# Moving the last rope-query transposes, the context's own attention and some due times in a one-core hybrid attention step

## The chip, the core and the metric

The kernel runs on one core of one Trainium2 chip. The metric is the device time of one execution in microseconds, here always called the time; the profile adds a span, which runs from the first to the last instruction of the program on that core. Five engines work side by side, each through a queue of its own in fixed order: TensorE (PE, with its weight loads as PEld), VectorE (DVE), ScalarE (ACT), GpSimd (POOL) and SyncE (SP), which here issues DMAs only.

## What is computed

One step of a diffusion trunk for 1024 latent tokens and 128 context tokens, all fp32, width 1024, one layer. Both token sets pass the same weights:

```python
h = _rmsnorm(x, norm_g) * (1 + scale) + shift           # scale, shift from the conditioning vector
u, v, g_a, c_q, c_kv, k_rope, g_b = _split_in(h @ w_in)
a_out = _chunk_mlp(u, v, w_s, b_s, g_v) * silu(g_a)      # gated mixing of positions, chunks of 128
q = (_rmsnorm(c_q, q_norm_g) @ w_uq)                     # 4 heads, 128 nope and 64 rope columns each
ckv = _rmsnorm(c_kv, kv_norm_g)                          # latent keys and values, 128 wide
attn = softmax over (1024 latent keys with rotated k_rope, 256 cached context keys unrotated)
y = concat([a_out, attn * silu(g_b)]) @ w_o
x = x + gate * y                                         # then a last rmsnorm
```

The context tokens attend only to themselves (one tile of 128 queries by 128 keys, four heads). The query of a head is kept as three pieces that are multiplied with the keys: the nope part folded with the key expansion, the rotated rope part and the raw rope part.

## The kernel before

Nine tiles of 128 tokens: tiles 0 to 7 are latent, tile 8 (`NS`) is the context. Every fp32 matrix product is done as three fp32r products (high by high, high by low, low by high), so each operand has a high half, made by an ACT or POOL cast, and a low half, made by a DVE subtraction (`lo_of`, L109). Nothing is scheduled by the machine here: instructions stand on each engine in the order in which the Python calls them, and the code steers that order with a clock of its own. `run((cost, fn))` (L204) calls a step and moves the clock by `cost`; `later(dt, fn)` (L164) puts a follow-up, such as an eviction, at a due time; `need(key)` (L194) pulls waiting follow-ups forward until a key is made; `merged(a, b)` (L209) interleaves two lists of steps by their costs.

The stages, by the time in the profile: from 0 to 246 us normalisation, modulation and the projections of group A and the gates; from 246 to 310 us the loop over tiles (L1044 to L1058) that projects `z` (c_q, c_kv, k_rope), with z's transposes, the folding of weights, rope queries and nope queries of earlier tiles beside it; from 310 to 322 us a hand-written list (L1074 to L1092) that closes this phase; from 322 to 508 us the attention; then the output projection.

The names that matter below. `zacc8` is the PSUM bank with z of tile 8. `cq_transpose(t)` (L927) transposes c_q of a tile into bank `cqT`; ACT writes the high half `cqh`, DVE the low half `cql`. `q_rope(t)` (L957) multiplies them with the rope weights into bank `qr`; ACT copies it out (`qun`), DVE and POOL rotate it (`qr1`). `q_rope_T(t)` (L983) transposes the result into bank `qrT` and splits it in two parts: ACT cast L1001, DVE subtraction L1002, for the even heads and for the odd ones. `keys(t0, n, kind)` (L1007) transposes latent keys (kind 0, `kch`, `kcl`) or rope keys (kind 1, `krh`, `krl`) of n tiles through bank `kT`. `q_nope` gives `qn`. Until 322 us PSUM is divided in a ring of six banks (`psa`) and a ring of two (`pst`); a new tile in a ring waits until the bank's last reader is done.

In the attention a head of a latent tile has three score steps: `lat(0)` and `lat(1)`, five matmuls of 512 columns each into `s1`, and `con`, five of 256 into `s2` (L1141 to L1145). DVE then takes the two maxima (L1116, L1119) and the shift (L1120), ACT the exponentials (L1126, two per head, each followed by a read-out of the row sum), DVE the reciprocal and POOL scales the row (L1132). `value_stream` transposes two heads' rows in five groups (`pT`, L1188, in the ring `pst` of two banks), splits them (ACT `ph`, L1192; DVE `pl`, L109) and multiplies them with the values into bank `o`.

The context's own attention is `own_steps()` with four steps: `score` (20 matmuls of 128 columns into `s8`), `tr` (four transposes of the scaled rows `e8` into `pT8`), `av` (three matmuls into `o8`) and `up` (the value expansion into `at8`, also from the ring `pst`). They are placed between the score steps of the first heads by hand:

```python
own = own_steps()
first = [s_ for i in range(LEAD) for s_ in score_steps(*heads[i])]
merged(first[:4] + own[:1] + first[4:], [])
...
    if c == 0:
        sc = sc[:3] + own[1:2] + sc[3:5] + own[2:3] + sc[5:] + own[3:]
```

With `LEAD = 2`, `first` holds heads 0 and 1 of tile 0; the loop's round `c` adds two more heads and, from round 1 on, the value stream of the pair of heads before.

Of the kernel before, what the change touches and what calls it, by code (L numbers as in the profile page):

```python
# [18 lines left out]
P = 128  # L19
NT = 9  # L20
NS = 8
# [70 lines left out]
def tile_hymba_step(ctx: ExitStack, tc: tile.TileContext, I, O):  # L92
# [777 lines left out]
    def z_stats(t, ps):  # L870
# [52 lines left out]
        later(0.35, squares)  # L923
        later(0.9, rope_key)
        later(1.5, scales)

    def cq_transpose(t):  # L927
        last = t == NT - 1
        ps = (psa if last else pst).tile([P, 512], F32, tag="acc" if last else "t", name=f"cqT{t}")
        for q in range(2):  # L930
            T.transpose(ps[:, q * P : (q + 1) * P], zt[t][:, q * P : (q + 1) * P], ident)
        src = ps[:, 0:256].rearrange("p (q c) -> p q c", q=2)
        dh = cqh[:, :, t * P : (t + 1) * P]

        def low():
            lo_of(cql[:, :, t * P : (t + 1) * P], src, dh)
            made.add(("cq", t))

        later(0.4, lambda: S.copy(dh, src))
        later(0.85, low)  # L940
# [14 lines left out]
    rot = {}  # L955

    def q_rope(t):  # L957
# [4 lines left out]
        un = zp.tile([P, 4, 64], F32, tag="qun", name=f"qun{t}", bufs=3)  # L962
        rot[t] = [un]

        def raw():
            S.copy(un, ps[:, :256].rearrange("p (h r) -> p h r", h=4))
# [3 lines left out]
            r1 = zp.tile([P, 4, 64], F32, tag="qr1", name=f"qr1{t}", bufs=2)  # L970
# [10 lines left out]
        later(0.85, raw)  # L981

    def q_rope_T(t):  # L983
# [3 lines left out]
        late = t == NS  # L987
# [19 lines left out]
    def keys(t0, n, kind):  # L1007
        need(*[("k", t0 + i) for i in range(n)])
        ps = (psa if t0 == 4 else pst).tile([P, 512], F32, tag="acc" if t0 == 4 else "t", name=f"kT{t0}{kind}")
        for i in range(n):  # L1010
            src = kvn[:, t0 + i, :] if kind == 0 else krd[:, t0 + i, :, :].rearrange("p a r -> p (a r)")
            T.transpose(ps[:, i * P : (i + 1) * P], src, ident)
        sl = slice(t0 * P, (t0 + n) * P)
        dh, dl = (kch, kcl) if kind == 0 else (krh, krl)
        later(0.11 * n + 0.1, lambda: S.copy(dh[:, sl], ps[:, : n * P]))
        later(0.25 * n + 0.3, lambda: lo_of(dl[:, sl], ps[:, : n * P], dh[:, sl]))
# [23 lines left out]
    with tc.manual_schedule(engines=engines):  # L1040
# [3 lines left out]
        for t in range(NT):  # L1044
# [21 lines left out]
        vl = kv.tile([P, 11, P], F32R, tag="vl", name="vl")  # L1066
        for i, (dh, dl) in enumerate(((kch, kcl), (krh, krl))):
# [3 lines left out]
        later(11.0, lambda: pool_copy(cv[0], ctxr[:, 2, :]))  # L1071
        later(11.0, lambda: G.tensor_tensor(cv[1], ctxr[:, 2, :], f32(cv[0]), op=ALU.subtract))
        for t0, c in ((8, 1), (0, 4), (4, 4)):
            later(11.5, lambda t0=t0, c=c: values(t0, c))  # L1074
        for cost, fn in (
# [8 lines left out]
            (1.05, lambda: q_nope(2, 0)),  # L1084
            (0.15, lambda: keys(8, 1, 1)),
            (0.15, lambda: keys(8, 1, 0)),
            (1.05, lambda: q_nope(2, 1)),
            (1.05, lambda: q_nope(2, 2)),
            (0.25, lambda: q_rope_T(8)),
# [322 lines left out]
    with tc.manual_schedule(engines=engines):  # L1412
# [28 lines left out]
        merged(first[:4] + own[:1] + first[4:], [])  # L1441
        for c in range(len(pairs)):
            sc = [s_ for i in (2 * c + LEAD, 2 * c + LEAD + 1) if i < len(heads) for s_ in score_steps(*heads[i])]
            if c == 0:
                sc = sc[:3] + own[1:2] + sc[3:5] + own[2:3] + sc[5:] + own[3:]
# [3 lines left out]
            if 2 * c + LEAD + 1 == 11:  # L1449
                c_wo, wo = opened("wo", side="left")  # L1450
# [211 lines left out]
```

## Time and profile before

| | us |
|---|---|
| time, median of 3 runs | 629.55 (629.07 to 630.03) |
| time of the profiled execution | 629.15 |
| its span | 627.2 |
| PE busy | 612.7 (98%) |
| DVE busy | 359.7 (57%) |
| ACT busy | 265.2 (42%) |
| POOL busy | 177.8 (28%) |

The page gives busy time by engine, the chain that ended last and the costliest groups; the trace behind it answers for a stretch of time, for one engine's instructions in order with the idle time before each, and for single tiles. The profiled execution's time is 0.40 us below the median of the runs, and 1.95 us above its own span, which is the work around the program. In a timeline row the first number is the start in us from the span's beginning, the second how long the row took; a row `x2` holds two instructions. Matmuls overlap: the next one starts before the row of the last has ended, so the pace of PE is read from start to start.

### The profile page before, as it was taken

To read this page: it belongs to the slowest core of one execution; us is meant where nothing else is said; L and a number is where in the kernel's file an instruction comes from. 1 tells how busy PE (TensorE), PEld (TensorE's weight loads), DVE (VectorE), ACT (ScalarE), POOL (GpSimd) and SP (SyncE) were. 2 spreads that over 40 slices of the span, in tenths; PEclk is the share of its full clock that TensorE was granted. 3 is DMA by queue.
4 is the path that set the end of the run, shared out by engine and by line. 5 is a ranking of instruction groups with operands and counts; after the bars stand their busy time and mean duration, and the time that the engine had idled before them with its cause. 6 is when DMAs were issued, how large, how long until landed. Compare 5 with 4: busy or idle time off the path is not lost.

```text
span 627.2 us, 9800 instructions
## 1 busy us (share of the span) xinstructions
PE 612.7 (98%) x3703; PEld 552.5 (88%) x3703; DVE 359.7 (57%) x839; ACT 265.2 (42%) x638; POOL 177.8 (28%) x217
## 2 busy tenths in 40 slices
PE   8999999999999999999989999999999999999995
PEld 7568889999999999999977999999999988888884
DVE  4773456049556100456677666776666754487655
ACT  8655753112111111565666555546656543132212
POOL 2551123344535500433444212332222341000001
PEclk9999999999999999999999999999999999999999
DMA  8992010042321203000010000001101123423311
GB/s 324 401 355 68 1 33 2 2 169 82 116 103 62 93 4 114 27 2 1 1 41 1 2 0 1 2 2 34 34 1 33 36 68 103 167 100 135 112 56 67
DMA packets 15966, 46.32 MB, mean 74 GB/s; under 512 B 1952, under 2 KB 4912, under 8 KB 15920
## 3 DMA queue, kind: packets, MB, share of 16 engines
q1 hardware_dynamic: 15776, 45.51, 20.6%
q8 instruction: 29, 0.48, 0.3%
q10 hardware_dynamic: 144, 0.20, 0.1%
q14 instruction: 17, 0.14, 0.1%
HBM read 40.87 MB, written 4.83 MB: 73 GB/s over the span
## 4 chain that ended last, share of the span: by engine, by line
PE 92%; DVE 3%; ACT 2%; DMA 1%; issue 1%; SPq 0%; ACTq 0%
PE tp L716 6%; PE tp L156 6%; PE tp L155 6%; PE tp L157 6%; PE pT L1188 5%; PE w L1435 5%; PE w L1436 5%; PE w L1437 5%; PE o L1212 3%; PE o L1214 3%; PE s L1141 3%; PE o L1213 3%; PE s L1143 3%; PE s L1144 3%; PE s L1142 3%; PE s L1145 3%
## 5 line engine op out<-in xcount | busy, mean ns | idle before, releaser
L109 DVE TENSOR_TENSOR pl<-pT,ph 128x512 fp32r<-128x512 f32 x81 | 55.5, 687 | 48.2 <-ACT ph L1192 48.0
L1132 POOL TENSOR_SCALAR e<-e,rs 128x1280 f32<-128x1280 f32 x32 | 42.8, 1338 | 137.5 <-DVE rs L1131 118.8
L157 PE MATMUL tp<-area,w2l 128*128 128x384 f32 x216 | 72.5, 336 | 0.0
L155 PE MATMUL tp<-area,w2h 128*128 128x384 f32 x216 | 72.5, 336 | 0.0
L156 PE MATMUL tp<-area,w2h 128*128 128x384 f32 x216 | 72.5, 336 | 0.0
L1126 ACT ACTIVATE e<-s,nb,scl 128x256 f32<-128x256 f32 x64 | 56.1, 880 | 36.5 <-DVE nb L1120 36.4
L1192 ACT CAST ph<-pT 128x512 fp32r<-128x512 f32 x80 | 45.3, 588 | 43.5 <-PE pT L1188 40.6
L1188 PE MATMUL pT<-ident,e 128*128 128x128 f32 x320 | 47.9, 272 | 0.6 <-DVE pl L109 0.6
L1212 PE MATMUL o<-ph,vh 128*128 128x256 f32 x160 | 47.8, 299 | 0.0
L109 DVE TENSOR_TENSOR w2l<-w2r,w2h 128x1024 fp32r<-128x1024 f32 x12 | 19.8, 1656 | 45.5 <-POOL w2h L112 45.5
L1214 PE MATMUL o<-ph,vl 128*128 128x256 f32 x160 | 44.9, 281 | 0.0
L1213 PE MATMUL o<-pl,vh 128*128 128x256 f32 x160 | 44.7, 280 | 0.0
L1437 PE MATMUL w<-area,ml 128*128 128x512 f32 (+1 forms) x114 | 43.2, 379 | 0.0
L1188 PEld LDWEIGHTS pT<-ident,e 128*128 128x128 f32 x320 | 37.5, 140 | 4.3 <-DVE pl L109 1.5
L155 PEld LDWEIGHTS tp<-area,w2h 128*128 128x128 f32 x216 | 40.5, 188 | 0.6 <-issue 0.5
L156 PEld LDWEIGHTS tp<-area,w2h 128*128 128x128 f32 x216 | 40.5, 188 | 0.2
L157 PEld LDWEIGHTS tp<-area,w2l 128*128 128x128 f32 x216 | 40.5, 188 | 0.0
L1116 DVE TENSOR_REDUCE m<-s 128x1 f32<-128x1024 f32 x32 | 38.9, 1216 | 2.3 <-PE s L1145 2.3
L1141 PE MATMUL s<-kch,area 128*128 128x512 f32 (+2 forms) x100 | 39.0, 390 | 0.1
L716 PE MATMUL tp<-area,w2h 128*128 128x384 f32 x144 | 37.4, 340 | 0.0
L1144 PE MATMUL s<-krh,area 128*128 128x512 f32 (+2 forms) x100 | 35.4, 354 | 0.0
L1143 PE MATMUL s<-kch,area 128*128 128x512 f32 (+2 forms) x100 | 35.4, 354 | 0.0
(308 smaller groups left out, 1576.0 us busy)
## 6 DMA issues: line engine op xcount, KB each, us to landing
ada<-in_ada_ss SPq DMA_DIRECT2D x16, 512.0 KB, 10.1
w2r<-in_w_t SPq DMA_DIRECT2D x12, 512.0 KB, 3.6
x<-in_x SPq DMA_DIRECT2D x9, 512.0 KB, 5.8
xr<-in_x SPq DMA_DIRECT2D x9, 512.0 KB, 4.6
adag<-in_ada_g SPq DMA_DIRECT2D x8, 512.0 KB
wor<-in_w_o SPq DMA_DIRECT2D x8, 512.0 KB, 3.4
out_y<-y SPq DMA_DIRECT2D x8, 512.0 KB, 2.7
wvr<-in_w_v SPq DMA_DIRECT2D x8, 256.0 KB, 8.9
```

Of the source, the lines that this page charges most:

```text
L109: V.tensor_tensor(lo, src, f32(hi), op=ALU.subtract)
L155: T.matmul(ps, wh, xh, start=j == 0, stop=False)
L156: T.matmul(ps, wh, xl, start=False, stop=False)
L157: T.matmul(ps, wl, xh, start=False, stop=j == n - 1)
L716: T.matmul(tps[i, g][:, :GW], w_[i][:, k, :], x_[k, g], start=k == 0 and j == 0, stop=k == NK - 1 and j == 2)
L1126: S.activation(e[:, sl], src, AF.Exp, bias=nb, scale=scl[:, t : t + 1], accum_out=su[:, i : i + 1])
L1141: T.matmul(ps, qh_, kch[:, sl], start=True, stop=False)
L1188: T.transpose(ps[:, w : w + P], es[t, h][:, c * P : (c + 1) * P], ident)
L1212: T.matmul(o, vh[:, kt, :], ph[:, sl], start=c == 0, stop=False)
L1213: T.matmul(o, vh[:, kt, :], pl[:, sl], start=False, stop=False)
L1214: T.matmul(o, vl[:, kt, :], ph[:, sl], start=False, stop=c == n - 1)
L1437: T.matmul(ps, b, woh[k][:, c0:c1], start=False, stop=k == NK - 1)
```

## The change

Five things are done; no arithmetic is added or taken away, and the number of instructions on PE, DVE and POOL stays the same.

1. In the loop over the z tiles, the c_q transposes, the weight fold and the rope-query transposes of a round become one step (`full`) in place of three that were spread among z's chunks.
2. The rope queries' transposes of tile 6 go from the closing list into the last round of that loop, those of tile 8 between the score steps of heads 0 and 1, and those of tile 7 into round 1 of the attention. The copies that they read, for tiles 7 and 8, get a pool of their own (`ra`), which is closed before the pool of the output weights is opened in its place; so the first load of output weights now also waits for POOL's last use of it.
3. `keys(0, 4, ·)` takes its banks from the ring of six in place of the ring of two.
4. Due times: for tile 8 the squares of z and what follows them come later; the c_q split of tile 8 is due sooner; the rope copies of tiles 7 and 8 are due later, the first low half of the keys too; the values' copies on POOL are due sooner.
5. The own attention: `score` goes from behind `lat(0)` of head 1 to behind all of head 1; `tr` stays behind head 2; `av` goes behind all of head 3; `up` goes behind `lat(0)` of head 4, into the round that also runs the first value stream.

```diff
         later(0.3, lambda: S.copy(zs, ps[:, :448]))
-        later(0.35, squares)
+        later(1.2 if t == NS else 0.35, squares)
         later(0.9, rope_key)
-        later(1.5, scales)
+        later(2.2 if t == NS else 1.5, scales)
...
-        later(0.4, lambda: S.copy(dh, src))
-        later(0.85, low)
+        later(0.05 if last else 0.4, lambda: S.copy(dh, src))
+        later(0.42 if last else 0.85, low)
...
-        later(0.85, raw)
+        later({7: 2.6, 8: 1.2}.get(t, 0.85), raw)
...
-        late = t == NS
+        late = t >= 7
         tp = (pst if late else psa).tile([P, 512], F32, tag="t" if late else "acc", name=f"qrT{t}")
...
-        ps = (psa if t0 == 4 else pst).tile([P, 512], F32, tag="acc" if t0 == 4 else "t", name=f"kT{t0}{kind}")
+        ps = (psa if t0 < 8 else pst).tile([P, 512], F32, tag="acc" if t0 < 8 else "t", name=f"kT{t0}{kind}")
...
+            full = []
             if t >= 1:
-                beside.append((0.25, lambda t=t: cq_transpose(t - 1)))
+                full.append((0.25, lambda t=t: cq_transpose(t - 1)))
             if 1 <= t < 5:
-                beside.append((0.45, lambda t=t: fold(t - 1)))
+                full.append((0.45, lambda t=t: fold(t - 1)))
             if t >= 3:
-                beside.append((0.45, lambda t=t: q_rope_T(t - 3)))
+                full.append((0.45, lambda t=t: q_rope_T(t - 3)))
+            if full:
+                beside.append((sum(f[0] for f in full), lambda full=full: [f[1]() for f in full]))
...
             if t == NT - 1:
+                beside.append((0.45, lambda: q_rope_T(t - 2)))
                 beside.append((0.75, lambda: q_rope(t - 1)))
...
-            (0.45, lambda: q_rope_T(6)),
-            (0.45, lambda: q_rope_T(7)),
             (0.75, lambda: q_rope(8)),
...
-            (0.25, lambda: q_rope_T(8)),
...
-        merged(first[:4] + own[:1] + first[4:], [])
+        merged(first[:3] + [(0.25, lambda: q_rope_T(8))] + first[3:] + own[:1], [])
...
             if c == 0:
-                sc = sc[:3] + own[1:2] + sc[3:5] + own[2:3] + sc[5:] + own[3:]
+                sc = sc[:3] + own[1:2] + sc[3:] + own[2:3]
+            if c == 1:
+                sc = sc[:1] + own[3:] + sc[1:4] + [(0.45, lambda: q_rope_T(7))] + sc[4:]
...
             if 2 * c + LEAD + 1 == 11:
+                closed(c_ra)
                 c_wo, wo = opened("wo", side="left")
```

Three places show what this does to the order of instructions. A digit behind a name is the tile, or the tile and the head (`e01` is head 1 of tile 0).

First TensorE, right behind the last matmul of z, in the kernel before: the keys' transposes, the c_q transposes of tile 8, the rope queries' transposes, then the rope query of tile 8.

```order
L1012 MATMUL kT00_3165<-ident_75,kvn_2366 128x128 x4
L1012 MATMUL kT01_3176<-ident_75,krd_2367 128x128 x4
L931 MATMUL cqT8_3190<-ident_75,z8_3142 128x128 x2
L1012 MATMUL kT40_3194<-ident_75,kvn_2366 128x128 x4
L1012 MATMUL kT41_3203<-ident_75,krd_2367 128x128 x4
L992 MATMUL qrT6_3218<-ident_75,qr16_3073 128x128 x2
L992 MATMUL qrT6_3218<-ident_75,qun6_3058 128x128 x2
L992 MATMUL qrT7_3225<-ident_75,qr17_3155 128x128 x2
L992 MATMUL qrT7_3225<-ident_75,qun7_3138 128x128 x2
L155 MATMUL qr8_3232<-wrh_2358,cqh_2354 128x256
```

The same place in the changed kernel:

```order
L1015 MATMUL kT00_3166<-ident_75,kvn_2366 128x128 x4
L1015 MATMUL kT01_3177<-ident_75,krd_2367 128x128 x4
L931 MATMUL cqT8_3187<-ident_75,z8_3149 128x128 x2
L1015 MATMUL kT40_3192<-ident_75,kvn_2366 128x128 x4
L1015 MATMUL kT41_3214<-ident_75,krd_2367 128x128 x4
L155 MATMUL qr8_3222<-wrh_2358,cqh_2354 128x256
```

Eight transposes have left: four went ahead of z's end, four into the attention.

Second ScalarE at the start of the attention, before: `e8` stands between the exponentials of heads 0 and 1, and the copy of `o8` between those of heads 2 and 3.

```order
L1126 ACTIVATE e00_3338,su00_3336<-s2_3320,nb00_3335,scl_92 128x256
L1126 ACTIVATE e00_3338,su00_3336<-s100_3323,nb00_3335,scl_92 128x1024
L1332 ACTIVATE e8_3386,su8_3389<-s8_3355,nb8_3388,scl_92 128x128 x4
L1126 ACTIVATE e01_3385,su01_3383<-s2_3320,nb01_3382,scl_92 128x256
L1126 ACTIVATE e01_3385,su01_3383<-s101_3345,nb01_3382,scl_92 128x1024
L1349 CAST ph8_3442<-pT8_3437 128x512
L1126 ACTIVATE e02_3427,su02_3425<-s2_3320,nb02_3424,scl_92 128x256
L1126 ACTIVATE e02_3427,su02_3425<-s102_3405,nb02_3424,scl_92 128x1024
L1366 COPY e8_3386<-o8_3466 128x512
L1126 ACTIVATE e03_3465,su03_3463<-s2_3320,nb03_3462,scl_92 128x256
L1126 ACTIVATE e03_3465,su03_3463<-s103_3446,nb03_3462,scl_92 128x1024
```

And in the changed kernel, up to the same pair of heads:

```order
L1133 ACTIVATE e00_3325,su00_3323<-s100_3310,nb00_3322,scl_92 128x1024
L1004 CAST area2_119<-qrT8_3332 64x2x128
L1133 ACTIVATE e01_3357,su01_3355<-s2_3307,nb01_3354,scl_92 128x256
L1133 ACTIVATE e01_3357,su01_3355<-s101_3337,nb01_3354,scl_92 128x1024
L1339 ACTIVATE e8_3399,su8_3402<-s8_3368,nb8_3401,scl_92 128x128 x4
L1356 CAST ph8_3436<-pT8_3431 128x512
L1133 ACTIVATE e02_3418,su02_3416<-s2_3307,nb02_3415,scl_92 128x256
L1133 ACTIVATE e02_3418,su02_3416<-s102_3393,nb02_3415,scl_92 128x1024
L1133 ACTIVATE e03_3459,su03_3457<-s2_3307,nb03_3456,scl_92 128x256
L1133 ACTIVATE e03_3459,su03_3457<-s103_3440,nb03_3456,scl_92 128x1024
L1373 COPY e8_3399<-o8_3469 128x512
L1199 CAST ph00_0_3489<-pT00_0_3484 128x512
```

The four exponentials of `e8` now stand behind both of head 1, the copy of `o8` behind both of head 3, and the second part of the rope queries of tile 8 (L1004; the first part stands two rows ahead of the piece) between heads 0 and 1. On DVE the maxima of head 1 likewise stand ahead of those of `s8`.

Third TensorE around the last step of the own attention, before: `at8` follows the `con` step of head 3, ahead of head 4.

```order
L1362 MATMUL o8_3466<-ph8_3442,vl_3153 128x512
L1141 MATMUL s2_3320<-kch_3148,area0_117 128x256
L1142 MATMUL s2_3320<-kcl_3149,area0_117 128x256
L1143 MATMUL s2_3320<-kch_3148,area0_117 128x256
L1144 MATMUL s2_3320<-krh_3150,area0_117 128x256
L1145 MATMUL s2_3320<-krl_3151,area0_117 128x256
L1375 MATMUL at8_3480<-e8_3386,wuv_2364 128x128 x4
L1141 MATMUL s110_3489<-kch_3148,area0_117 128x512
```

And now:

```order
L1195 MATMUL pT00_1_3491<-ident_75,e00_3325 128x128
L1195 MATMUL pT00_1_3491<-ident_75,e01_3357 128x128
L1382 MATMUL at8_3499<-e8_3399,wuv_2364 128x128 x4
L1195 MATMUL pT00_2_3510<-ident_75,e00_3325 128x128
L1195 MATMUL pT00_2_3510<-ident_75,e01_3357 128x128
```

`at8` now stands behind the first half of head 4's scores and behind the first two groups of transposes of the value stream (`pT00_0`, four transposes, stands just ahead of this piece, and `pT00_1` begins with two more like the first two rows); `pT00_0`, `pT00_1` and `at8` follow each other in the ring of two banks. `s110` is the first half of head 4.

More of the change, by code (lines that the diff above doesn't have):

```diff
@@ L1070, in tile_hymba_step @@
         cv = [v_[:, 9:, :].rearrange("p a r -> p (a r)") for v_ in (vh, vl)]
[L1071 to L1072 removed]
+        later(9.0, lambda: pool_copy(cv[0], ctxr[:, 2, :]))
+        later(9.0, lambda: G.tensor_tensor(cv[1], ctxr[:, 2, :], f32(cv[0]), op=ALU.subtract))
         for t0, c in ((8, 1), (0, 4), (4, 4)):
[L1074 removed]
+            later(9.5, lambda t0=t0, c=c: values(t0, c))
         for cost, fn in (
```

15 lines of the change are left out of this document (10 added, 5 removed).

## The prediction

> **What bounds the kernel now.** I read the page first, then the busy time by stretches, then TensorE's timeline where it was not full. In the second fence the columns are the stretch, its length, and the busy time (with instruction counts) of PE, PEld, DVE, ACT and POOL, then the granted clock.
>
> ```profile
> PE 612.7 (98%) x3703; PEld 552.5 (88%) x3703; DVE 359.7 (57%) x839; ACT 265.2 (42%) x638; POOL 177.8 (28%) x217
> ```
>
> ```profile
> 246.00:310.00 64.00, 63.99 (x368) 59.85 (x367) 35.64 (x117) 34.40 (x103) 21.92 (x61) 1.00 0.04 10
> 310.00:346.00 36.00, 32.76 (x200) 27.90 (x200) 26.02 (x58) 23.14 (x58) 16.12 (x22) 1.00 0.06 19
> 346.00:480.00 134.00, 134.00 (x935) 123.56 (x934) 90.75 (x190) 76.61 (x159) 36.01 (x33) 1.00 0.03 11
> ```
>
> TensorE sets the end: it is full while z is projected and full in the attention, and short by 3.24 us between 310 and 346, where the change works. Work that merely changes its place on a full TensorE costs nothing, and a microsecond in which TensorE waits is a microsecond at the end. So the sum is one of waits. Those of TensorE in that stretch stand in brackets:
>
> ```profile
> 313.89 0.39 PE L155 MATMUL qr<-wrh,cqh 128*128 128x256 f32 x1 [0.18 <-ACT cqh L939]
> 315.36 0.39 PE L157 MATMUL qr<-wrh,cql 128*128 128x256 f32 x1 [0.96 <-DVE cql L109]
> 320.81 0.44 PE L992 MATMUL qrT<-ident,qun 128*128 128x128 f32 x2 [1.16 <-DVE krl L109]
> 322.40 0.50 PE L1141 MATMUL s<-kch,area 128*128 128x512 f32 x1
> 338.47 1.16 PE L1375 MATMUL at<-e,wuv 128*128 128x128 f32 x8 [0.42 <-ACT e L1366]
> 343.23 0.66 PE L1188 MATMUL pT<-ident,e 128*128 128x128 f32 x4 [0.41 <-DVE pl L109]
> ```
>
> That is 0.18 + 0.96 + 1.16 + 0.42 + 0.41 = 3.13 us: it is the most that this stretch can give, 0.5% of the time. The first matmul after a wait also takes about 0.1 us longer than its like, which I count with each wait.
>
> **The front, 310 to 322 us.** With the rope queries' transposes gone, TensorE still stops at the third matmul of the rope query of tile 8, which needs `cql` from DVE.
>
> ```profile
> 312.60 0.49 ACT L888 ACTIVATE zw<-ssz,epsb 128x1 f32<-128x1 f32 x2
> 312.99 0.58 ACT L1015 CAST krh<-kT 128x512 fp32r<-128x512 f32 x1
> 313.45 0.39 ACT L939 CAST cqh<-cqT 128x256 fp32r<-128x256 f32 x1
> 310.33 0.37 ACT L966 COPY qun<-qr 128x256 f32<-128x256 f32 x1 [1.50 <-PE qr L157]
> ```
>
> ```profile
> 310.80 0.42 DVE L975 TENSOR_TENSOR qr<-qr,rope 128x256 f32<-128x256 f32 x1 [0.93 <-ACT qun L966]
> 314.89 0.41 DVE L109 TENSOR_TENSOR cql<-cqT,cqh 128x256 fp32r<-128x256 f32 x1
> ```
>
> Before, the cast `cqh` starts at 313.45, behind two roots (312.60 to 312.99) and `krh` (to 313.45). Now those 0.85 us stand behind it, while four transposes of tile 6 (about 0.11 us each, row of eight at 340.63 below) delay z's end by 0.43: `cqh` starts at 313.03. But on DVE the rotation of tile 7 now stands ahead of `cql`, and it waits for the copy `qun`, which stands behind `cqh` (0.39) and `krh` (0.46): 313.88, plus 0.47 from copy to rotation as above, plus 0.42, plus 0.41 for `cql`: 315.18, and TensorE at 315.24 instead of 315.36. The new wait for the bank of z of tile 8, at `kT41`, for which the late squares answer, ends before that and adds nothing.
>
> From there to the first score before: 322.40 − 315.36 = 7.04. Of it go the wait of 1.16, 0.22 for the transposes of tile 8, about 0.1 of idle time ahead of the first score and about 0.1 of restart. The first score starts at 315.24 + 5.46 = 320.70, 1.7 us earlier. Of that 0.65 (six transposes) is only put off, and the first score's own restart of 0.1 goes too. Net **−1.15**. Ends: −1.6 if rows overlap as closely as `zw` and `krh` do, −0.7 if DVE loses another half.
>
> **The rope query of tile 8, now inside the attention.** Its two parts are split by ACT and DVE; the first and last rows give the shorter form (64x256) as their least duration, the longer (64x512) as their median, in ns.
>
> ```profile
> L1001 ACT CAST area<-qrT x18: 366/582/597, 269.4 to 321.7; 64x512 fp32r<-64x512 f32 x16, 64x256 fp32r<-64x256 f32 x2
> L1002 DVE TENSOR_TENSOR area<-qrT,area x18: 419/685/694, 272.1 to 322.8; 64x512 fp32r<-64x512 f32 x16, 64x256 fp32r<-64x256 f32 x2
> ```
>
> ```profile
> 328.59 0.19 ACT L1126 ACTIVATION_READ_ACCUMULATOR e<-s,nb,scl 128x1 f32 x1
> ```
>
> ```profile
> 325.43 0.40 PE L1141 MATMUL s<-kch,area 128*128 128x512 f32 x1
> 326.57 0.22 PE L1141 MATMUL s<-kch,area 128*128 128x128 f32 x1
> ```
>
> I keep the clock of before, with the first score at 322.40. Head 0's exponentials end with the read-out at 328.59; the next ACT row can start at about 328.69, and that is now the second part: 0.37, then DVE 0.42 and 0.42: 329.53 and 329.95 with 0.05 of handing over. TensorE now has, ahead of `s8`, the other half of head 1 (326.57 − 325.43 = 1.14), its `con` (0.62, from 2.90 for a head as below less two halves) and 0.22 of transposes: `s8` starts at 328.55 and its first rope matmul, the fourth, at 328.88. It waits until 329.59: **+0.7**, and 0.1 of restart. The cover that hid these splits before was the nope queries; who waits behind the matmul is all of the attention. Ends 0.5 and 0.95.
>
> **The chain from `s8` to `e8`.** The rows that it is made of:
>
> ```profile
> 329.81 0.15 DVE L1130 TENSOR_TENSOR rs<-su 128x1 f32<-128x1 f32 x1
> ...
> 330.17 1.23 DVE L1116 TENSOR_REDUCE m<-s 128x1 f32<-128x1024 f32 x1
> ```
>
> ```profile
> 330.07 0.46 ACT L1332 ACTIVATE e<-s,nb,scl 128x128 f32<-128x128 f32 x1 [1.29 <-issue]
> ...
> 332.02 0.56 ACT L1126 ACTIVATE e<-s,nb,scl 128x256 f32<-128x256 f32 x1
> ...
> 333.66 0.19 ACT L1126 ACTIVATION_READ_ACCUMULATOR e<-s,nb,scl 128x1 f32 x1
> ```
>
> ```profile
> 328.64 0.28 PE L1145 MATMUL s<-krl,area 128*128 128x128 f32 x1
> ...
> 330.57 0.40 PE L1141 MATMUL s<-kch,area 128*128 128x512 f32 x1
> ...
> 333.47 0.60 PE L1346 MATMUL pT<-ident,e 128*128 128x128 f32 x4
> ```
>
> In the kernel before, the chain from the last matmul of `s8` (328.64) to `pT8` (333.47) takes 4.83 us, and TensorE is covered by one and a half heads. Now one head stands between them: 333.47 − 330.57 = 2.90. Even an undisturbed chain leaves a wait of 4.83 − 0.11 − 2.90 = 1.8. And it is disturbed: DVE, free at 329.95, takes head 0's two small rows (330.17 − 329.81 = 0.36) and head 1's maxima ahead of those of `s8`; from the first maximum to head 1's exponentials are 332.02 − 330.17 = 1.85, so these start at 332.16 and hold ACT until about 333.9 (1.74 from 332.02, with the 0.19 of the read-out half overlapped). From the first exponential of `e8` to `pT8` are 333.47 − 330.07 = 3.40, through ACT, a reciprocal and POOL: `pT8` at 337.3. TensorE gets there at 329.59 + 0.1 + 1.78 (sixteen matmuls) + 2.90 = 334.4. Wait **+2.9**, restart 0.1. I take the disturbed chain, since every step has its row; ends 1.8 and 3.1.
>
> **The last step, `at8`.**
>
> ```profile
> 334.10 0.59 ACT L1349 CAST ph<-pT 128x512 fp32r<-128x512 f32 x1 [0.24 <-PE pT L1346]
> ...
> 337.84 0.58 ACT L1366 COPY e<-o 128x512 f32<-128x512 f32 x1
> ...
> 341.87 1.06 ACT L1192 CAST ph<-pT 128x512 fp32r<-128x512 f32 x2
> ```
>
> ```profile
> 342.49 1.29 DVE L109 TENSOR_TENSOR pl<-pT,ph 128x512 fp32r<-128x512 f32 x2
> ```
>
> ```profile
> 340.63 1.04 PE L1188 MATMUL pT<-ident,e 128*128 128x128 f32 x8
> ```
>
> `pT00_0`, `pT00_1` and `at8` share two banks, so `at8` waits until DVE has read `pT00_0`. Count from the start of `pT8`, called C. TensorE: restart 0.1, `pT8` 0.44, head 3's two halves 2.29, `con` 0.6, `o8` 0.7, half a head 1.14, two groups of transposes 0.88 (1.04 for eight, less the tail): `at8` is reached at C + 6.15. ACT: the cast of `pT8` at C + 0.63 (334.10 − 333.47), 0.5, then head 2's exponentials 1.75: C + 2.9; DVE's two small rows 0.36, head 3's maxima and shift until its exponentials 1.85: C + 5.1; 1.75 for them, 0.5 for the copy of `o8`: C + 7.35, where `ph` of `pT00_0` begins; `pl` begins 0.62 later (342.49 − 341.87) and takes 0.69: C + 8.7. Wait **+2.55** with 0.1 of restart. The waits of 0.42 and 0.41 that this place had go, with 0.2 of restart: net **+1.6**. Even without any queue: 0.62 + 0.69 + the transposes' tail of 0.27, less 0.44 of cover, is a wait of 1.1; so ends +0.2 and +2.1 net.
>
> **The transposes of tile 7 in round 1.**
>
> ```profile
> 348.69 1.23 DVE L1116 TENSOR_REDUCE m<-s 128x1 f32<-128x1024 f32 x1 [0.17 <-PE s L1145]
> ...
> 353.55 0.69 DVE L109 TENSOR_TENSOR pl<-pT,ph 128x512 fp32r<-128x512 f32 x1 [2.44 <-ACT ph L1192]
> ...
> 354.83 0.60 PE L1188 MATMUL pT<-ident,e 128*128 128x128 f32 x4
> ```
>
> They bring two DVE parts of 0.69 each, and with them one `pl` of 0.69, ahead of head 5's maximum (348.69), which had waited only 0.17: its chain shifts by about 1.8. It ends in the `pl` at 353.55, whose bank the transposes at 354.83 need: slack 354.83 − 354.24 = 0.59, and 0.44 more by the transposes themselves. Wait **+0.75**, with 0.1 of restart; ends 0 and 1.3.
>
> **The rest at nothing.** The three steps in one among z's chunks: TensorE is full from 246 to 310 with or without it, and in both kernels work follows at once. The values' copies on POOL come sooner, hidden by the attention's first rounds, since the first who reads them is `o8`. The first load of output weights on SP waits for the pool `ra`; behind it are only the other output weights, first used by TensorE after 480 us, and the cover is some 100 us.
>
> **Sum** against the profiled execution's 629.15: −1.15 + 0.8 + 3.0 + 1.6 + 0.85 = **+5.1**, so 634.25 by the profile's own time. That time is 0.40 below the median of 629.55; against the median the forecast is 634.7.
>
> **The rivals.** *The waits stay hidden, faster.* The front gains 1.15 and the old waits at `at8` and behind it go (1.03); if `pT8` and `at8` met ready operands, the rope split alone would stay: −1.15 − 1.03 + 0.8 = −1.4, 628.2. It decides at `pT8`: the chain from `s8` would have to fit into 3.0 us. Against it stand 4.83 measured and two rows put ahead of it. 4 in 100.
>
> *The front does not do what it says.* The late squares hold z's bank and the rotation of tile 7 stands ahead of `cql`; if the first score comes only by the wait of 1.16 less the put-off transposes, say −0.3 instead of −1.15, the time is 635.6. For it: the new position gains only 0.12 at `cql` in my sum. 12 in 100.
>
> *The clock falls in the new waits.* TensorE would run slower after the two long ones.
>
> ```profile
> 619.00:622.00 3.00, 0.71 (x6) 0.50 (x5) 1.88 (x6) 0.80 (x2) 0.96 (x1) 1.00 0.00 0
> 622.00:624.00 2.00, 0.00 (x0) 0.00 (x0) 1.26 (x5) 0.62 (x1) 0.00 (x0) 1.00 0.00 0
> 624.00:625.00 1.00, 0.00 (x0) 0.00 (x0) 0.00 (x0) 0.00 (x0) 0.00 (x0) 0.88 0.66 257
> ```
>
> At the end of this trace TensorE stops at 619.7, and the granted clock is still full at 624; a mean of 0.88 in the next microsecond is a fall to half at 624.76, 5 us after the last matmul. Waits of 2.9 and 2.55 are shorter. Should it fall, a head's 2.90 us at half clock costs 2.9 more: 637.6. 4 in 100. The Trainium skill, "TensorE: Matmul & The Clock Gate", section "HAM oscillation", speaks against such gaps: idle time of TensorE over about 3.4 us halves its clock. By that rule, too, neither wait is long enough, and with it the margin would be 0.5 us instead of 2; the trace shows no gap between the two figures.
>
> *No change.* All four new waits at their low ends (0.6 + 1.9 + 0.2 + 0) less 1.6 give +1.1. 3 in 100.
>
> **The numbers.** My forecast has 77 in 100. Low ends of all terms but the front's give 631.1, high ends of all 636.6, and the second rival lies within; the range 631.2 to 636.8 takes these in and leaves out the faster case, most of the no-change case and the clock. Below 0.2% (1.26 us) a measurement of this kernel cannot tell a change from none. Faster 0.04, the same 0.03, slower 0.93.
>
> **What would show it.** In the changed profile TensorE should wait at `pT` (L1353) for POOL's `e` by 2 to 3 us, at `at` (L1382) for DVE's `pl` by 2 to 3, at the rope matmul of `s8` (L1151) for DVE by 0.5 to 1, near 359 us at `pT` by up to 1.3, and no longer at `qrT`; the first score should start near 320.7. Were the first two waits under 1 us, the forecast would be wrong, and so it would be if TensorE lost the time in z's loop.

## The result, and the profile after

The changed kernel takes 638.19 us (median of 6 runs, 636.67 to 640.66), the kernel before 629.79 beside it (6 runs, 629.07 to 631.68): ratio 1.0133, 95% interval 1.0116 to 1.015. It is slower, as forecast, but by 8.4 us and not by 5, and so above the range. The profiled execution took 638.04 us, its span is 636.0.

Since the start of the program differs from run to run (below, with the hardware), I compare stretches between two events that every version has: from the first matmul of z's projection to the end of the last matmul. In TensorE's timeline of the kernel before:

```profile
246.19 0.36 PE L1032 MATMUL zacc<-qh,area 128*128 128x448 f32 x1
...
619.43 0.28 PE L1437 MATMUL w<-area,ml 128*128 128x256 f32 x1
```

And after, with the waits between them in brackets:

```profile
246.19 0.36 PE L1035 MATMUL zacc<-qh,area 128*128 128x448 f32 x1
...
313.22 0.66 PE L1015 MATMUL kT<-ident,krd 128*128 128x128 f32 x4 [0.39 <-ACT j L879]
...
315.03 0.38 PE L157 MATMUL qr<-wrh,cql 128*128 128x256 f32 x1 [0.92 <-DVE cql L109]
...
320.32 0.39 PE L1148 MATMUL s<-kch,area 128*128 128x512 f32 x1
...
327.43 0.33 PE L1151 MATMUL s<-krh,area 128*128 128x128 f32 x1 [0.71 <-DVE area L1005]
...
336.08 1.12 PE L1353 MATMUL pT<-ident,e 128*128 128x128 f32 x4 [3.42 <-POOL e L1346]
...
345.89 2.08 PE L1382 MATMUL at<-e,wuv 128*128 128x128 f32 x8 [2.21 <-DVE pl L109]
...
363.17 0.66 PE L1195 MATMUL pT<-ident,e 128*128 128x128 f32 x4 [1.42 <-DVE rs L1137]
...
627.83 0.28 PE L1444 MATMUL w<-area,ml 128*128 128x256 f32 x1
```

The stretch is 619.71 − 246.19 = 373.52 us before and 628.11 − 246.19 = 381.92 after: 8.40 more. Every wait that the prediction named is there, at its place and with its releaser (the last one, at 363.17 instead of near 359, is put down to `rs`, which on DVE comes right behind the predicted `pl`; that `pl` ends at 363.11). But the waits do not add up to the loss. The first score comes 2.08 earlier, of which 0.65 (six transposes) is put off: −1.43. The four waits are 0.71 + 3.42 + 2.21 + 1.42 = 7.76, the old ones of 0.42 and 0.41 are gone: with the front together 5.50, and about 0.2 for restarts. That is 5.7 of 8.4. The busy time by stretches has the rest (columns: stretch, length, busy PE, PEld, DVE, ACT, POOL, granted clock, DMA):

```profile
332.10:335.51 3.41, 0.56 (x5) 0.35 (x3) 1.11 (x4) 2.59 (x10) 1.86 (x2) 1.00 0.00 0
335.51:338.93 3.42, 2.85 (x9) 2.47 (x10) 1.74 (x4) 1.70 (x4) 0.51 (x1) 0.50 0.00 0
342.34:345.75 3.41, 1.33 (x11) 0.97 (x9) 0.93 (x4) 3.25 (x7) 0.99 (x1) 1.00 0.00 0
345.75:349.17 3.42, 3.28 (x14) 3.19 (x15) 1.37 (x3) 0.32 (x1) 0.34 (x1) 0.50 0.02 5
359.41:362.82 3.41, 2.34 (x16) 1.93 (x14) 0.93 (x3) 2.75 (x7) 0.00 (x0) 1.00 0.00 0
```

The granted clock is 0.50 in two stretches of 3.41 us, one around the end of each long wait. They begin 10.24 us apart, three times 3.41, and each follows a stretch of that length in which TensorE was busy for 0.56 or 1.33 us of 3.41 (0.16 and 0.39 of it). The shorter wait near 363 us leaves 2.34 (0.69), and the clock stays. Inside such a stretch a 128x512 matmul starts 0.42 us after the one ahead of it, outside 0.23; in TensorE's timeline after:

```profile
337.85 0.63 PE L1150 MATMUL s<-kch,area 128*128 128x512 f32 x1
338.27 0.63 PE L1151 MATMUL s<-krh,area 128*128 128x512 f32 x1
...
339.04 0.39 PE L1148 MATMUL s<-kch,area 128*128 128x512 f32 x1
339.27 0.39 PE L1149 MATMUL s<-kcl,area 128*128 128x512 f32 x1
```

Work that took 2.85 and 3.28 us at half clock would take half of it at full clock: up to 1.4 + 1.6 = 3.1 us, which covers what the waits leave open. In z's loop and behind 372 us nothing has changed: TensorE is full from 246 to 310 us and from 372 to 480 us in both.

### The profile page after: what moved, and what is told of

Read it like the earlier page. It is cut to its first block, busy times and chain, and to the rows that moved or that the text cites. A ratio compares the mean times of both kernels' runs of the same rounds, so it can differ in the third digit from the quotient of the medians.

```text
span 636.0 us, 9803 instructions
## 1 busy us (share of the span) xinstructions
PE 614.1 (97%) x3703; PEld 554.4 (87%) x3703; DVE 362.8 (57%) x839; ACT 264.1 (42%) x638; POOL 174.7 (27%) x217
```

## The experiments

Theory A: the new waits cost their own length, and each of the two long ones half a clock for the next 3.41 us besides. Its rivals: B, the clock has no price of its own; C, not the own attention's new places but the rope transposes inside the attention cost the time. Later a theory D on the size of the longest wait. "Stretch" is the one defined above, from each run's own profile, which is a single execution. The runs 1 to 4, 5 to 8, and 9 and 10 were made on three chips; the kernel before that stands beside them ran on the same one.

| version | stretch, us | against before | median, us | before beside it | ratio (95%) |
|---|---|---|---|---|---|
| before | 373.52 | | 629.79 | | |
| changed | 381.92 | +8.40 | 638.19 | 629.79 | 1.0133 (1.0116 to 1.015) |
| 1 waits filled | 379.35 | +5.83 | 636.32 | 630.18 | 1.0101 (1.0086 to 1.0115) |
| 2 own attention alone | 378.76 | +5.24 | 636.04 | 630.18 | 1.0099 (1.0085 to 1.0112) |
| 3 own attention back | 373.54 | +0.02 | 631.23 | 630.18 | 1.0012 (1.0001 to 1.0024) |
| 4 at8 back | 379.28 | +5.76 | 635.63 | 630.18 | 1.009 (1.0076 to 1.0104) |
| 5 combined | 372.14 | −1.38 | 628.44 | 631.01 | 0.9964 (0.995 to 0.9977) |
| 6 tile 8's rope query back | 378.81 | +5.29 | 637.28 | 631.01 | 1.0099 (1.0086 to 1.0113) |
| 7 tile 7's rope query early | 378.17 | +4.65 | 635.98 | 631.01 | 1.0082 (1.0067 to 1.0096) |
| 8 waits half filled | 379.34 | +5.82 | 636.32 | 631.01 | 1.0085 (1.007 to 1.01) |
| 9 later normalization | 380.96 | +7.44 | 638.03 | 630.77 | 1.0118 (1.0105 to 1.0132) |
| 10 combined, later normalization | 371.17 | −2.35 | 628.89 | 630.77 | 0.9962 (0.9949 to 0.9976) |

**1, the waits filled.** Matmuls that nobody reads, 12 ahead of pT8's transposes and 7 ahead of at8:

```diff
+            for _ in range(12):
+                T.matmul(ps, qnh[0][:, 0, :P], kch[:, :512], start=True, stop=True)
+            for _ in range(7):
+                T.matmul(filled["s"][:, 1, :], qnh[0][:, 0, :P], kch[:, :512], start=True, stop=True)
```

> The changed kernel with matmuls that nobody reads (128x512, 0.23 us each in this trace) put on TensorE where it waits: 12 of them (2.75 us) ahead of pT8's transposes, into their bank, and 7 (1.6 us) ahead of at8, into a half of head 4's scores that is overwritten later. The steps that the waits wait for are not touched. Theory A (each of the two long waits leaves one stretch of 3.41 us nearly empty, and the next 3.41 us run at half clock): the waits shrink to about 0.7 and 0.6 but pT8 and at8 start when they did, the granted clock stays 1.00 throughout, and the 2.85 and 3.28 us of work that lay in the two stretches of half clock take half as long: 3.1 us less, 635.1. Theory B (all of the loss is the waits themselves and what stands behind them in the queues; the slow matmuls are not from the clock or the clock falls for another reason): 638.2 or more, the clock at 0.5 as before.

TensorE's timeline of this run:

```profile
336.69 0.55 PE L1356 MATMUL pT<-ident,e 128*128 128x128 f32 x3 [0.67 <-POOL e L1347]
...
345.50 0.71 PE L1387 MATMUL at<-e,wuv 128*128 128x128 f32 x4 [0.92 <-DVE pl L109]
```

Its busy time by stretches, at the places where the clock had fallen:

```profile
337.91:341.33 3.42, 3.42 (x19) 2.92 (x18) 2.24 (x5) 1.81 (x5) 1.05 (x1) 1.00 0.00 0
...
344.74:348.15 3.41, 2.65 (x18) 2.44 (x19) 2.38 (x4) 1.04 (x2) 0.96 (x1) 1.00 0.00 0
```

Theory A holds and B falls: 19 more matmuls, and 2.57 us less. The gain is smaller than the 3.1 expected for a reason that the rows show. Counted from z's first matmul, pT8 starts at 89.9 us in both, but at8 only 1.0 earlier (98.7 against 99.7), not 1.4: it waits for ACT's and DVE's chain behind head 3, and part of what TensorE gains it waits out again (0.92, and 1.6 of filling). The second stretch of half clock is worth the other 1.55.

**2, the own attention alone.** The kernel before, with the own attention's steps in their new places and nothing else:

```diff
-        merged(first[:4] + own[:1] + first[4:], [])
+        merged(first + own[:1], [])
-                sc = sc[:3] + own[1:2] + sc[3:5] + own[2:3] + sc[5:] + own[3:]
+                sc = sc[:3] + own[1:2] + sc[3:] + own[2:3]
+            if c == 1:
+                sc = sc[:1] + own[3:] + sc[1:]
```

> The kernel before, and of the change only the new places of the steps of tile 8's own attention (its scores behind head 1, at8 in round 1). The rope queries of tiles 7 and 8 stay ahead of the attention, as before. Theory A: a wait at pT8 between 1.8 (undisturbed chain) and 2.9, a wait at at8 of 2.2, the old waits of 0.42 and 0.41 gone, and half clock behind at8 (1.6) and perhaps behind pT8 (1.4): 5 to 7 us more than before, 635 to 637. Theory C (what costs is the rope queries' transposes inside the attention, with their splits on ACT and DVE ahead of the maxima; the new places of the own attention are nearly hidden): at most 1.4 us more, below 631.2, and waits under 1 us.

The two waits in TensorE's timeline, and the stretches around them:

```profile
337.62 0.55 PE L1346 MATMUL pT<-ident,e 128*128 128x128 f32 x3 [2.35 <-POOL e L1339]
...
346.42 0.90 PE L1375 MATMUL at<-e,wuv 128*128 128x128 f32 x3 [2.51 <-DVE pl L109]
```

```profile
332.92:336.33 3.41, 2.35 (x13) 1.85 (x11) 0.85 (x5) 3.32 (x12) 1.20 (x1) 1.00 0.00 0
336.33:339.75 3.42, 2.13 (x12) 1.82 (x13) 2.47 (x5) 1.43 (x4) 1.17 (x2) 1.00 0.00 0
...
343.16:346.57 3.41, 0.90 (x8) 0.67 (x7) 1.22 (x4) 2.97 (x7) 1.28 (x1) 1.00 0.00 0
346.57:349.99 3.42, 3.42 (x15) 3.23 (x16) 1.18 (x3) 0.58 (x1) 0.05 (x1) 0.50 0.02 5
```

C falls: the new places alone cost 5.24. (The rope queries' transposes have a price too while the own attention stands there, as runs 6 and 7 show.) And the two waits show that it is not the length of a wait that decides on the clock. The wait of 2.35 lies across the border of two stretches, which keep 0.69 and 0.62 of their time busy, and the clock stays; that of 2.51 lies in one stretch, leaves 0.26 of it, and the clock falls.

**3, the own attention back**, the reverse: the changed kernel with the own steps in their old places, and tile 8's rope query two steps earlier, behind `lat(0)` of head 0.

```diff
+        merged(first[:1] + [(0.25, lambda: q_rope_T(8))] + first[1:4] + own[:1] + first[4:], [])
+                sc = sc[:3] + own[1:2] + sc[3:5] + own[2:3] + sc[5:] + own[3:]
+                sc = sc[:1] + sc[1:4] + [(0.45, lambda: q_rope_T(7))] + sc[4:]
```

> The changed kernel with the own attention's four steps back in their old places; the rope query of tile 8 is still transposed inside the attention (one half of a head after the first score instead of three steps), that of tile 7 still in round 1. Theory A: the waits at s8's rope matmul, pT8 and at8 go, those of before at at8 and behind it (0.42 and 0.41) come back, the clock stays at 1.00; left are the front's gain (first score 2.1 us earlier, 0.65 of it put off) and round 1's wait of 1.4: 629.6 to 630.3. Theory C: the rope transposes inside the attention still cost their waits: 633 or more.

The loss is gone: the stretch is 373.54, as before. The waits that are left are 0.44 and 0.43 at the old places and 0.19 and 0.73 in round 1 (TensorE's timeline), and the clock stays. The median of 631.23 is above the expected 629.6 to 630.3, but before's beside it is higher too (630.18), and in the profiled execution (631.8) z's first matmul comes at 248.26, 2.07 later than in the profile before; that arises in the first 20 us and is told with the hardware below.

**4, only at8 back**, at the end of round 0:

```diff
+                sc = sc[:3] + own[1:2] + sc[3:5] + own[2:3] + sc[5:] + own[3:]
+                sc = sc[:1] + sc[1:4] + [(0.45, lambda: q_rope_T(7))] + sc[4:]
```

> The changed kernel with only the last step, at8, back at the end of round 0. pT8's wait of 3.4 and the half clock behind it stay. Theory A: the wait of 2.21 goes for one of about 0.4, and the half clock behind it with it (1.6): 3.0 to 3.6 less, 634.6 to 635.2, one stretch of 3.41 us at half clock left. Theory B (no price of the clock apart from the wait): 1.8 less, 636.4.

Behind the same wait of 3.42 at pT8 the stretches are now:

```profile
331.03:334.44 3.41, 1.56 (x9) 0.97 (x7) 1.06 (x4) 3.41 (x12) 0.93 (x1) 1.00 0.00 0
334.44:337.85 3.41, 1.84 (x7) 1.65 (x8) 1.85 (x5) 0.87 (x4) 1.45 (x2) 0.50 0.00 0
337.85:341.27 3.42, 3.42 (x10) 2.65 (x9) 1.00 (x3) 1.65 (x4) 1.21 (x1) 0.50 0.00 0
```

The stretch loses 2.64, not 3.0 to 3.6. at8's wait and its half clock went as A says, and round 1's wait is 0.19 and 0.71 instead of 1.42. But the borders lie elsewhere in this run: the wait takes up part of two stretches, the first is left with 0.46, the second (already at half clock) with 0.54, and TensorE runs at half clock for 6.83 us instead of 3.41. The same wait costs more or less by where the borders fall. B's 636.4 lies at the top of the runs (634.49 to 636.38), so this run alone does not decide between A and B; the first does.

**5, combined.** The changed kernel's front, the own attention's old places, tile 8's rope query behind `lat(0)` of head 0, tile 7's in round 0:

```diff
+        merged(first[:1] + [(0.25, lambda: q_rope_T(8))] + first[1:4] + own[:1] + first[4:], [])
+                sc = sc[:2] + [(0.45, lambda: q_rope_T(7))] + sc[2:3] + own[1:2] + sc[3:5] + own[2:3] + sc[5:] + own[3:]
+                sc = sc
```

> The changed kernel's front, with the own attention's four steps in their old places, the rope query of tile 8 transposed one half of a head after the first score and that of tile 7 in round 0, half a step ahead of pT8. Theory A: no long wait is left; of the front's 2.08 us, 0.65 goes to the six transposes that are only put off, and of the old waits of 0.42 and 0.41 the second is covered by the new transposes: from the first matmul of z's projection to the last matmul of all 371.8 to 372.5 us, against 373.52 in the profile before, so about 0.2% faster. Against it (theory C: the rope splits inside the attention cost wherever they stand): tile 7's two DVE parts of 0.69 push e8's chain back, a wait of about 1.4 at pT8: 373.5 or more, no gain.

372.14, and 0.9964 of the kernel before: faster than both. The front's gain is real, and it can be kept. One wait of 1.25 is left, at o8 for DVE (experiment 10).

**6, tile 8's rope query back** in the closing list, ahead of the last nope query, all else as changed:

```diff
+            (0.25, lambda: q_rope_T(8)),
+        merged(first + own[:1], [])
```

> The changed kernel with only the rope query of tile 8 transposed in the closing list again, ahead of the last nope query. Theory A, with the disturbed chain of the prediction: s8's wait of 0.71 and its restart go, and since the split no longer stands ahead of head 0's small rows and head 1's maxima on DVE, pT8's wait falls from 3.4 to about 2.4, as in the run with the own attention alone; together 1.8 less, and up to 1.4 more or less by whether the half clock follows: 380 us from z's first matmul to the last of all (381.9 in the changed profile), 635 to 637. Against it: the chain to pT8 does not depend on the split, so pT8's wait takes over what s8's wait gives: less than 0.5 us gained.

TensorE's timeline, and the stretch with pT8's wait and the one behind it, where the clock stayed:

```profile
336.23 0.55 PE L1354 MATMUL pT<-ident,e 128*128 128x128 f32 x3 [2.36 <-POOL e L1347]
```

```profile
334.50:337.91 3.41, 1.68 (x10) 1.47 (x11) 2.15 (x5) 1.33 (x5) 1.60 (x2) 1.00 0.00 0
337.91:341.32 3.41, 3.41 (x19) 2.89 (x18) 2.34 (x6) 1.34 (x4) 1.33 (x1) 1.00 0.00 0
```

s8's wait is gone and pT8's is 2.36 instead of 3.42, as in run 2: the split of tile 8's rope query costs its own 0.7 and about 1 us more in the chain to pT8. A wait of 2.36 that leaves 0.49 of its stretch does not bring the half clock, which falls behind at8 only; so the stretch is 3.11 shorter, near the upper end of what was expected (1.8, and up to 1.4 more). The median of 637.28 is above the expected 635 to 637; in the profile z begins 2.15 later than in that of before. The small DVE row that run 9 is about is held in runs 2 and 6 as well (1.16 each), so this 1 us is not the one found there.

**7, tile 7's rope query early**, in round 0 ahead of pT8:

```diff
+                sc = sc[:2] + [(0.45, lambda: q_rope_T(7))] + sc[2:3] + own[1:2] + sc[3:] + own[2:3]
+                sc = sc[:1] + own[3:] + sc[1:]
```

> The changed kernel with only the rope query of tile 7 transposed in round 0, half a head ahead of pT8, and not in round 1. Theory A: the wait of 1.42 near 363 us goes with its restart, and the four transposes (0.44) now run inside pT8's wait: 1.9 less, 380.0 us from z's first matmul to the last of all, about 636.3. Against it: its two DVE parts of 0.69 stand in e8's chain instead, pT8's wait grows by 1.0 or more, and little or nothing is gained.

pT8 in TensorE's timeline of this run:

```profile
337.22 0.55 PE L1353 MATMUL pT<-ident,e 128*128 128x128 f32 x3 [3.13 <-POOL e L1346]
```

The wait in round 1 is gone with its price. pT8's wait is 3.13: 0.44 of it is covered by the transposes, and the chain is 0.15 later, not 1.0. The stretch is 3.75 shorter, 1.9 as expected; most of the rest is the half clock, which in this run fell behind pT8 only (at8's wait of 1.89 leaves 0.55).

**8, the waits half filled**, with 8 and 3 matmuls.

> As the run with filled waits, but with 8 and 3 matmuls instead of 12 and 7, so that waits of about 1.6 and 1.8 us stay. Theory A, with a threshold: in the profiles so far a stretch of 3.41 us was followed by half clock when TensorE was busy for 0.46 of it or less, and not from 0.50 on; one idle time of 1.6 to 1.7 leaves 0.50 to 0.53 wherever the stretches begin, one of 1.8 leaves 0.47 at worst, so the clock should stay at 1.00, or fall once in a few runs: 379.3 us from z's first matmul to the last of all, as with the waits filled further. Theory B' (any wait over about 1 us brings the half clock): 381 to 382.

The stretches around the waits of 1.58 (pT8) and 1.83 (at8):

```profile
334.71:338.12 3.41, 1.91 (x11) 1.65 (x12) 2.38 (x5) 1.33 (x6) 1.37 (x2) 1.00 0.00 0
338.12:341.54 3.42, 3.42 (x19) 2.87 (x18) 2.15 (x6) 1.23 (x3) 1.33 (x1) 1.00 0.00 0
341.54:344.95 3.41, 1.64 (x12) 1.16 (x10) 1.01 (x4) 3.18 (x7) 1.06 (x1) 1.00 0.00 0
344.95:348.37 3.42, 3.36 (x24) 3.14 (x25) 2.40 (x5) 0.59 (x1) 0.27 (x1) 1.00 0.02 5
```

The clock stays at 1.00 and the stretch is that of run 1 (379.34 and 379.35), with 1.8 us more of idle time. A is right on the threshold too: about half of a stretch busy is enough. It also says that filling is no gain in itself; only the clock is.

**9, a later normalization.** This run asks why pT8's wait is 3.42 and not the 2.9 of the prediction. DVE's timeline of the changed kernel, ahead of head 1's exponentials, and POOL's:

```profile
329.37 0.41 DVE L1126 TENSOR_REDUCE m<-s 128x1 f32<-128x256 f32 x1
329.81 1.20 DVE L1127 SCALAR_TENSOR_TENSOR nb<-m,nscl 128x1 f32<-128x1 f32 x1
```

```profile
329.66 1.35 POOL L1139 TENSOR_SCALAR e<-e,rs 128x1280 f32<-128x1280 f32 x1 [6.81 <-PE s L1152]
```

The shift of head 1, a row of one column whose median over the 32 in this trace is 0.22, takes 1.20 and ends at 331.01, as POOL's normalization of head 0 does. The trace of before has one such row too, the shift of head 2, which ends at 336.07, 0.01 behind POOL's normalization of head 1:

```profile
334.73 1.33 POOL L1132 TENSOR_SCALAR e<-e,rs 128x1280 f32<-128x1280 f32 x1 [1.40 <-ACT ph L1349]
...
334.91 1.16 DVE L1120 SCALAR_TENSOR_TENSOR nb<-m,nscl 128x1 f32<-128x1 f32 x1
```

This run issues the normalization of head 0 later:

```diff
-            later(1.9, divide)
+            later(4.0 if (t, h) == (0, 0) else 1.9, divide)
```

> The changed kernel with the normalization of head 0 (two small rows on DVE and 1.35 us on POOL) issued later, behind the shift of tile 8's own scores. In the changed profile DVE's shift of head 1 took 1.20 us instead of 0.22 and ended at the same 331.01 us as POOL's row that had begun 0.15 ahead of it. Theory D (a DVE row on SBUF data that begins inside POOL's row is held to its end, and that is why pT8's wait was 3.42 and not 2.9 or less): the shift takes 0.22, head 1's exponentials begin 0.9 to 1.0 earlier, pT8's wait falls to about 2.45, and the time by 1.0 (and by the half clock behind pT8 in some runs): 380.9 us or less from z's first matmul to the last of all. Against it (the shift was late for its operands): the wait stays between 3.2 and 3.5 and nothing is gained.

DVE, POOL and TensorE in this run:

```profile
331.73 0.22 DVE L1127 SCALAR_TENSOR_TENSOR nb<-m,nscl 128x1 f32<-128x1 f32 x1
...
333.91 0.71 DVE L1137 TENSOR_TENSOR rs<-su 128x1 f32<-128x1 f32 x1 [0.83 <-ACT e L1133]
```

```profile
333.28 1.34 POOL L1139 TENSOR_SCALAR e<-e,rs 128x1280 f32<-128x1280 f32 x1 [8.16 <-DVE rs L1138]
335.08 1.34 POOL L1139 TENSOR_SCALAR e<-e,rs 128x1280 f32<-128x1280 f32 x1 [0.46 <-DVE rs L1138]
336.38 1.04 POOL L1346 TENSOR_TENSOR e<-e,rs 128x512 f32<-128x512 f32 x1
```

```profile
337.47 0.69 PE L1353 MATMUL pT<-ident,e 128*128 128x128 f32 x2 [2.69 <-POOL e L1346]
```

The shift takes 0.22 and the wait falls by 0.73, not by 1.0: the late normalization now holds another small row (`rs`, 0.71 instead of 0.15, ending at 334.62 with POOL's row), and e8 queues behind two normalizations on POOL. D holds, its remedy gives only part. The stretch is 0.96 shorter; the medians (638.03, with 630.77 for the kernel before beside it) do not contradict that, but cannot show it.

**10, combined, with head 1's normalization behind head 2's shift:**

```diff
-            later(1.9, divide)
+            later(2.6 if (t, h) == (0, 1) else 1.9, divide)
```

> The combined version (old places of the own attention, the front of the changed kernel) with the normalization of head 1 issued behind the shift of head 2. In its profile TensorE waited 1.25 at o8 for DVE, whose shift of head 2 took 1.17, ending with POOL's row. Theory D: that shift takes 0.22, the wait falls to 0.3 or goes (0.25 may come up at at8), 371.1 to 371.5 us from z's first matmul to the last of all, about 0.35 to 0.5% below the kernel before. Against it: the wait stays, 372.1.

o8 in TensorE's timeline of this run:

```profile
337.05 0.50 PE L1368 MATMUL o<-pl,vh 128*128 128x512 f32 x1 [0.32 <-DVE pl L109]
```

The wait is 0.32 instead of 1.25, and the stretch 371.17, the shortest of all. Against the kernel before the ratio is 0.9962, which the measurement does not tell from that of run 5.

## Why the prediction was wrong

The direction, the places and the releasers were right; the size was not. The step that failed is the one that put aside the rival "The clock falls in the new waits", with 4 in 100. It read from the tail of the trace that the clock falls 5 us after the last matmul, and concluded that "waits of 2.9 and 2.55 are shorter". Run 1 shows what that left out: 2.6 of the 8.4 us. With the clock held up, the kernel loses 5.83 in the stretch, against a sum of 5.1 for the whole change; so the sum was nearly the answer to run 1, not to the change. That the rival's own price, 2.9 for one head at half clock, lies near the measured 2.57 is luck: there were two falls, over stretches that were in part idle.

The tail of the same trace could have warned. There the matmuls end at 619.71, and the clock falls at 624.76 in the prediction's reading. Taken in stretches of 3.41 us that end there, in the busy time of the kernel before, TensorE was busy for 1.79 us of the last but one, and for nothing of the last:

```profile
617.92:621.34 3.42, 1.79 (x15) 1.58 (x14) 1.80 (x7) 1.66 (x3) 1.29 (x2) 1.00 0.00 0
621.34:624.75 3.41, 0.00 (x0) 0.00 (x0) 1.65 (x6) 0.82 (x2) 0.33 (x1) 1.00 0.13 49
```

So the 5 us are the rest of a stretch that was half full and one empty stretch; they belong to one position of the borders and are not the idle time that it takes. In run 1 the matmuls end at 626.16, and the clock falls at 628.05, 1.9 us later, behind a stretch of which 0.45 was busy. The Trainium skill, "TensorE: Matmul & The Clock Gate", Part 1 on the clock gate, gives the window of 3413 ns and says that it runs freely; the traces agree (335.51 and 345.75 are 3.00 such windows apart). The rule of its section "HAM oscillation", no idle gaps over about 3.4 us, which the prediction used, is not strict enough here: waits of 2.21 and 2.51 us brought the fall, and one of 2.35 did not.

Point by point, with run 1's and the changed kernel's rows:

- *Front:* first score at 320.32 against 320.70, a gain of 2.08 − 0.65 = 1.43 against 1.15. The wait for `cql` ends at 315.03 instead of 315.24, and the nope queries follow more closely. The wait of 0.39 for z's bank came and ended before that, as said.
- *s8's rope matmul:* 0.71 against 0.7. Its further price, about 1 us in the chain to pT8, was within the disturbed chain.
- *pT8:* 3.42 against 2.9, outside the ends of 1.8 and 3.1. The step "from the first maximum to head 1's exponentials" was taken from a row of before at 1.85; in the changed order POOL's normalization of head 0 falls on the shift in it, 0.98 more (run 9). The prediction took the step from head 1, whose shift was free in before; that of head 2, behind two small rows as in the changed order, was held there too. The Trainium skill, "SBUF — State Buffer", section "Who interferes with whom", has it as a rule: a DVE instruction with two inputs in SBUF contends with a GpSimd one that reads SBUF. The trace agrees, 1.20 instead of 0.22.
- *at8:* 2.21 against 2.55. At full clock it is 0.92 + 1.6 = 2.5 (run 1): the half clock ahead of it had hidden part of the wait.
- *Tile 7 in round 1:* 1.42 against 0.75 and outside the ends 0 and 1.3, in the way described. DVE stood still for ACT's part first, and head 5's maximum began about 2.3 late instead of 1.8.
- *The rest at nothing:* TensorE stayed full in z's loop and from 372 us on, as said.
- *The faster rival* needs no waits at pT8 and at8. Runs 5 and 10 are that case, by another order: with the own attention in its old places the front's gain is left.

## What to carry to other kernels

Price a wait of TensorE twice: by its length, and by what it does to the clock, which goes by the busy share of fixed stretches of 3.41 us and not by the wait alone. The falls behind the two long waits cost another 1.0 and 1.55 us (run 1); the two stretches at half clock in run 4 cost 2.6 by estimate, half of their busy 1.84 and 3.42. Waits of 2.2 to 3.4 us brought a fall, one of 2.35 and one of 2.36 did not; that depends on where the borders lie, and they lie elsewhere in each profile. Where a wait can't be removed, work that keeps its stretch half busy saves the clock. And a chain copied from a trace holds only while no POOL row on SBUF data comes to lie on its small DVE rows (1.20 us instead of 0.22).

## What the runs showed of the hardware

- **The clock's threshold.** In these profiles each full stretch of 3.41 us in the attention that TensorE was busy for 0.46 of it or less was followed by half clock (0.16, 0.26, 0.35, 0.39, 0.40, 0.41, 0.41, 0.46); those with 0.48, 0.49 and more were not. In the load phase it is less clear: of two stretches with 0.51, that of run 10 was followed by half clock, that of the changed kernel was not. The busy shares rest on modelled ends of matmuls, so the third digit means nothing. To come back from half clock took more: a stretch at half clock that was busy for 0.54 of it stayed there (run 4), those with 0.81 and more went back to full. What takes it back is not settled by this: at the start of run 3 (below) one with 0.96 did not, nor did those of runs 2 and 9 with 0.98 and 1.00, while run 10's with 1.00 did.
- **Transposes count as work.** This stretch of the changed kernel holds nearly only transposes (15 of its 18 matmuls), and the clock did not fall behind it:

```profile
311.62:315.03 3.41, 2.11 (x18) 1.63 (x16) 1.86 (x7) 3.38 (x13) 2.90 (x7) 1.00 0.02 5
```

- **The same effect has a part in the spread between runs.** In the first 20 us TensorE waits for loads, and in some runs a stretch there is too empty. In run 3 (TensorE only; length, busy, clock, DMA):

```profile
9.09:12.51 3.42, 1.28 (x16) 1.00 1.03 414
12.51:15.92 3.41, 3.29 (x16) 0.50 1.02 419
15.92:19.34 3.42, 3.42 (x12) 0.50 1.02 414
```

Two stretches at half clock follow one that is busy for 0.37, and z begins at 248.26. In the four profiles with such a stretch (runs 2, 3, 9 and 10) z begins 1.65 to 2.27 us later than in the profile before. It is not the only cause: in run 6, without one, z begins 2.15 later, in run 7 1.17, and in the other five profiles between 0.10 earlier and 0.62 later. The runs of the kernel before beside these experiments go the same way: those with a mean clock of 0.996 to 0.998 took 628.4 to 630.9 us, those with 0.992 and 0.993 630.4 to 631.9; of the 12 runs of version 3, the five with 0.996 or more took 629.07 to 630.70 us, the seven with 0.992 631.15 to 631.80. A difference of 0.2% can be hidden by this spread in the medians; a stretch that begins behind the load phase leaves it out, though each profile is one execution only.
